# Attention values as unsplit float32 products in the two column halves of the array, 512 queries at a time

## The chip, the cores and the metric

The kernel runs on one core of one Trainium2 chip. The metric is the device time of one execution in microseconds (us); the time before is the median of three runs, 1407.62 us, with 1405.22 us the lowest and 1408.63 us the highest. One further execution was recorded by the hardware profiler, and every row below is from that recording.

## What is computed

One layer of a streaming encoder, for 1024 new frames of one stream (the prompt, `T` = 1024) and for 32 next frames of a running stream (the sample, with 512 cached frames). Cut to the part that the change touches:

```
q, k, v = projections of rmsnorm(x), 16 heads of 64 channels; q and k normed per head
s = q @ k.T + (C[query] - C[key])           # C: cumulative log forget gates
s = where(query >= key, s, -inf); p = softmax(s)
o = p @ v                                    # per head, float32
ya = (o * silu(ga)) @ w_pa                   # beside it: a convolution branch, two gates, w_out
```

The prompt's attention is causal: query block i (128 queries) sees key blocks 0 to i. The running frames attend to the 512 cached keys and their own 32. The projections of q, k, v, of the gates (`ga`, `gb`, `ma`, `mb`) and of the convolution inputs (`ua`, `ub`) are the greater part of the work.

## The kernel before

**Number format.** TensorE is fed with numbers of a reduced float32 format (`F32R`). A float32 operand is split into a high part, rounded to that format, and a low part, the difference. A projection is then three products per tile (high by high, low by high, high by low; `mms`, L97 to L103, all on L102). A few products use plain float32 operands: the running frames' (L541, L860, L861, L895, L897), the column sums (L216, L995) and all transposes.

**Stages.** Up to about 610 us the kernel projects u, v, k, q and `ga` and writes them to scratch in device memory. From there to 1100 us it runs attention (the stretch that the change is about), with 22 of the 24 remaining gate projections between the attention steps as filler (`fill`, `filler`). The rest runs two more gates and then the three output projections.

**Values of the prompt, made once.** In the loop at L575 a 128-token block of v for four heads comes out of PSUM. ScalarE copies it twice: to `vf` (L588, written to the output `vO`) and to the high half of `vb` (L590). Three beats later VectorE forms the low half (`low`, L594), and SyncE writes `vb` to the scratch `s_v` (L597). So `s_v` holds, for each head, 64 high and 64 low columns side by side.

**One attention head.** `Head.load` (L770) loads q and k. `load_v` (L787) loads the head's 8 key blocks of `[high | low]` values into the one buffer `V`; for heads after the first it is called in the main loop when block 7 of the head before is done (L1050). A head is eight blocks; each block goes through three steps:

- `scores` (L906): products of queries and keys into PSUM, the row maximum on VectorE (L922), the exponential on ScalarE (L925), the scaling by the row sum on GpSimd (L928).
- `turn` (L930): up to 8 TensorE transposes (L945) of 128 by 128 pieces of P into PSUM, up to four to a PSUM buffer `ptr2`; then ScalarE casts the buffer to `pth` (high, L949) and VectorE subtracts to get `ptl` (low, L950). Two query blocks share a pair of tiles of 256 queries; GpSimd zeroes the corner above the diagonal in each (L935, L936).
- `values` (L952), only after odd blocks: with the 128 columns `[high | low]` of V as the stationary operand, the 256 queries of `pth` and then of `ptl` stream past, over 2, 4, 6 or 8 key blocks (L961, L962). The upper and the lower 64 rows of `po` are two partial sums; ScalarE copies one (L966), VectorE adds the other (L967), and for odd heads multiplies by the gate (L972) and the result is written to `s_o`.

The transposes and `po` draw on the same three PSUM buffers (`psT`).

**Order.** In attention the order of TensorE's instructions is the order of the program text (`manual_schedule`); the other engines' order is the scheduler's. The main loop (L1035) does, for step n of the list of blocks: scores of step n+3; loads for n+5; `turn` of n; `fill(4)`, that is 12 filler products; `values` of step n-2 if one is due.

**The running frames.** Four `Sample` steps, of four heads each, stand in the list. `Sample.values` (L888) multiplies, for each of its four heads j in turn, four cached key blocks (L895) and the 32 new keys (L897): plain float32, 64 stationary columns, 32 queries, into rows 0 to 63 of PSUM for even j and 64 to 127 for odd j.

Of the kernel before, what the change touches and what calls it, by code (L numbers as in the profile page):

```python
# [15 lines left out]
D = 1024  # L16
# [32 lines left out]
def build(tc, xT, xt, wv, wf, ckT, cv, clT, stT, vec, cst, yT, kT, vO, lfO, cpT, csT):  # L49
# [10 lines left out]
    s_v = dram.tile([8, 128, H, 128], F32, name="s_v")  # L60
# [17 lines left out]
    def f32(ap):  # L78
        return ap.bitcast(F32)
# [481 lines left out]
    for c in range(4):  # L561
        if c == 2:
            pace["rate"] = R_U
            u_proj(2, pj)
            while ("y", 0) not in sides or len(taps) > 62:
                pump(1)

            def shifted():
                shift_of(sides["y", 0])
                taps[:0] = sums(0)  # L570

            later(6, shifted)
        pace["rate"] = R_V
        wh2, wl2 = split.pop(("v", c))
        for t in range(8):  # L575
            ps = pj.tile([128, 512], F32, name="pjv", tag="pj")
            n = 0
            for kt in range(KT):
                sl = slice(t * 128, t * 128 + 128)
                wh, wl = wh2[kt // 4][:, kt % 4, :], wl2[kt // 4][:, kt % 4, :]  # L580
                for a, b in ((xh[:, kt, sl], wh), (xl[:, kt, sl], wh), (xh[:, kt, sl], wl)):
                    nc.tensor.matmul(ps[:, :VC], a, b, start=(n == 0), stop=(n == 23))  # L582
                    n += 1
                beat()
            if t == 2:
                fetch()
            vf = vp.tile([128, 256], F32, name="vf", tag="vf", bufs=6)
            nc.scalar.copy(vf, ps[:, :256])  # L588
            vb = vp.tile([128, 4, 128], F32R, name="vb", tag="vb", bufs=5)
            nc.scalar.copy(vb[:, :, 0:64], ps[:, :256].rearrange("p (h d) -> p h d", h=4))  # L590
            nc.scalar.copy(z[:, t, 4 * c:4 * c + 4], ps[:, 256:260])
            nc.sync.dma_start(vO[t * 128:t * 128 + 128, 256 * c:256 * c + 256], vf)

            def low(ps=ps, vb=vb, t=t, c=c):  # L594
                nc.vector.tensor_sub(vb[:, :, 64:128], ps[:, :256].rearrange("p (h d) -> p h d", h=4),
                                     f32(vb[:, :, 0:64]))
                nc.sync.dma_start(s_v[t, :, 4 * c:4 * c + 4, :], f32(vb))  # L597

            later(3, low)
    pvw.close()  # L600

    fp = pool("fp", 1, stack=pv, side="right")
# [163 lines left out]
    class Head:  # L766
# [3 lines left out]
        def load(self):  # L770
            h = self.h
            self.q = [hp.tile([n, T], F32R, name=a, tag=a) for a, n in (("QA", 68), ("QB", 128), ("KA", 68),
                                                                        ("KB", 128))]
            QA, QB, KA, KB = self.q
            hs = slice(64 * h, 64 * h + 64)
            nc.sync.dma_start(f32(QB[0:64]), s_q[1, hs, :])
            nc.sync.dma_start(f32(QB[64:128]), s_q[0, hs, :])
            nc.sync.dma_start(f32(KB[0:64]), s_k[0, hs, :])
            nc.sync.dma_start(f32(KB[64:128]), s_k[1, hs, :])
            nc.sync.dma_start(f32(QA[0:64]), s_q[0, hs, :])  # L780
            nc.sync.dma_start(f32(QA[64:68]), s_aq[h])
            nc.sync.dma_start(f32(KA[0:64]), s_k[0, hs, :])
            nc.sync.dma_start(f32(KA[64:68]), s_ak[h])
            if h == 0:
                self.load_v()

        def load_v(self):  # L787
            h = self.h
            self.V = hp.tile([128, 8, 128], F32R, name="V", tag="V", bufs=1)
            nc.sync.dma_start(f32(self.V), s_v[:, :, h, :].rearrange("b t d -> t b d"))  # L790

    cvt[0] = u7p
    pace["rate"] = R_U
# [44 lines left out]
    class Sample:  # L838
# [49 lines left out]
        def values(self):  # L888
            vc, vn, pts, g = self.vc, self.vn, self.pts, self.g
            po = psT.tile([128, 512], F32, name="po", tag="T")  # L890
            for j in range(4):
                b0 = 64 * (j % 2)
                o = po[b0:b0 + 64, 32 * (j // 2):32 * (j // 2) + 32]
                for b in range(4):
                    nc.tensor.matmul(o, vc[:, b, 64 * j:64 * j + 64], pts[:, b, 32 * j:32 * j + 32],  # L895
                                     start=(b == 0), stop=False)
                nc.tensor.matmul(o, vn[:, 64 * j:64 * j + 64], pts[:TS, 4, 32 * j:32 * j + 32], start=False, stop=True)  # L897
            nc.vector.tensor_copy(os_t[:, 2 * g:2 * g + 2, :], po[:, :64].rearrange("p (a n) -> p a n", a=2))

    class Block:  # L900
# [28 lines left out]

        def turn(self):  # L930
            i, P = self.i, self.P
            if i % 2 == 0:
                tg = f"{(i // 2) % 2}"
                pth, ptl = [ap.tile([128, i + 2, 256], F32R, name=a, tag=a + tg, bufs=1) for a in ("pth", "ptl")]
                nc.gpsimd.memset(f32(pth[:, i + 1, 0:128]), 0.0)  # L935
                nc.gpsimd.memset(f32(ptl[:, i + 1, 0:128]), 0.0)  # L936
                self.head.p = pth, ptl
            self.p = self.head.p
            pth, ptl = self.p
            qo = slice((i % 2) * 128, (i % 2) * 128 + 128)  # L940
            for u in range((i + 4) // 4):
                nj = min(4, i + 1 - 4 * u)
                pt = psT.tile([128, 512], F32, name="ptr2", tag="T")
                for j in range(nj):
                    nc.tensor.transpose(pt[:, 128 * j:128 * j + 128],  # L945
                                        P[:, 128 * (4 * u + j):128 * (4 * u + j) + 128], ident)
                p3 = pt[:, :128 * nj].rearrange("p (j q) -> p j q", j=nj)
                js = slice(4 * u, 4 * u + nj)
                nc.scalar.copy(pth[:, js, qo], p3)  # L949
                nc.vector.tensor_sub(ptl[:, js, qo], p3, f32(pth[:, js, qo]))  # L950

        def values(self):  # L952
            if self.i % 2 == 0:
                return
            c, e = self.i // 2, self.head.h % 2
            pth, ptl = self.p
            V, ot = self.head.V, self.head.ot
            njb = 2 * c + 2
            po = psT.tile([128, 512], F32, name="po", tag="T")
            for j in range(njb):  # L960
                nc.tensor.matmul(po[:, :256], V[:, j, :], pth[:, j, :], start=(j == 0), stop=False)  # L961
                nc.tensor.matmul(po[:, :256], V[:, j, :], ptl[:, j, :], start=False, stop=(j == njb - 1))  # L962
            osl = slice(c * 256, c * 256 + 256)
            own = slice(64 * e, 64 * e + 64)
            oth = slice(64 - 64 * e, 128 - 64 * e)
            nc.scalar.copy(ot[own, osl], po[oth, :256])  # L966
            nc.vector.tensor_add(ot[own, osl], ot[own, osl], po[own, :256])  # L967
# [5 lines left out]
            if e == 1 and c == 3:  # L973
                nc.sync.dma_start(s_o[self.head.h // 2, :, :T], ot)

    seq = []
    for h in heads:
        seq += [Block(h, i) for i in range(8)]
# [56 lines left out]
    for n, b in enumerate(seq):  # L1035
        if n + 3 < len(seq):
            start(seq[n + 3])
        if n + 5 < len(seq) and getattr(seq[n + 5], "i", 1) == 0:
            seq[n + 5].head.load()
        if n + 6 < len(seq) and isinstance(seq[n + 6], Sample):  # L1040
            seq[n + 6].load()
        if isinstance(b, Sample):
            fill(4)
            b.turn()
        else:
            b.turn()
# [219 lines left out]
```

## Time and profile before

| | |
|---|---|
| Runs | 1407.62 us median of 3 (1405.22 to 1408.63) |
| Span of the profiled execution | 1405.2 us, mean granted TensorE clock 0.998 |
| Busy share of the span: PE, DVE, ACT, POOL | 99%, 67%, 45%, 44% |
| Attention, 610 to 1100 us of the span | PE 486.4 of 490.0 us, DVE 329.0, ACT 266.3, POOL 177.8 |
| Device memory | 142 GB/s over the span, 201 MB |

The page gives the span of the profiled execution, 1405.2 us, and no other time for it; the median of the runs is 2.4 us above the span. PE is TensorE's matmul queue, PEld its loads of stationary operands, DVE VectorE, ACT ScalarE, POOL GpSimd, SP SyncE, whose queue issues the transfers. The duration of a matmul in a row includes its way through the array, in which the next one has already started: what a matmul costs a full TensorE is the distance from its start to the next one's. In an operand such as `128*64 128x32`, the first pair is the rows and columns of the array that are used, the second the streaming operand (rows by columns). In a timeline, neighbouring instructions of one line that touch are merged into one row with their count.

### The profile page before, as it was taken

How to read it: one execution, taken by the hardware profiler on the slowest of the kernel's cores; microseconds unless marked ns; L12 is line 12 of the kernel's file. 1: busy time of each engine (PE TensorE's matmuls, PEld its weight loads, DVE VectorE, ACT ScalarE, POOL GpSimd, SP SyncE). 2: the span in 40 equal slices, each digit the busy share in tenths (PEclk: the TensorE clock that was granted, in tenths of full speed). 3: DMA queues.
4: the chain of work that ended last, by engine and by line, in shares of the span. 5: the costliest groups of instructions: out<-in, count | busy, mean ns of one | idle time of the engine just before them, and what ended most of it. 6: DMA issues, size and time to landing. Idle time of an engine off the chain costs nothing.

```text
span 1405.2 us, 24570 instructions
## 1 busy us (share of the span) xinstructions
PE 1393.8 (99%) x9255; PEld 1363.2 (97%) x9255; DVE 936.7 (67%) x1407; ACT 637.7 (45%) x1308; POOL 624.3 (44%) x665
## 2 busy tenths in 40 slices
PE   9999999999999999999999999999999999999999
PEld 8999999999999999999999999999999999999998
DVE  6688787888898999567677767755565487133111
ACT  6332334645464642255545656654554456232100
POOL 2324254557585875344333434333432267255320
PEclk9999999999999999999999999999999999999999
DMA  4253443424342483343546546453542688444431
GB/s 181 92 178 114 153 134 101 159 84 136 110 146 95 143 200 120 129 123 103 147 123 175 160 138 175 115 164 110 171 132 82 231 286 285 146 138 142 150 108 47
DMA packets 110614, 201.23 MB, mean 143 GB/s; under 512 B 17376, under 2 KB 74592, under 8 KB 110496
## 3 DMA queue, kind: packets, MB, share of 16 engines
q1 hardware_dynamic: 110352, 199.60, 45.4%
q8 instruction: 73, 1.20, 0.4%
q14 instruction: 45, 0.37, 0.1%
q10 hardware_dynamic: 144, 0.07, 0.0%
HBM read 129.78 MB, written 69.84 MB: 142 GB/s over the span
## 4 chain that ended last, share of the span: by engine, by line
PE 93%; DVE 3%; issue 2%; ACT 2%; POOL 1%; ACTq 0%; DVEq 0%; POOLq 0%
PE pj L102 68%; PE pjv L582 7%; PE ptr L945 4%; PE po L961 3%; PE po L962 3%; PE psS L917 2%; PE psS L918 2%; DVE nm L922 1%; PE po L895 1%; PE warm L345 1%; PE pst L706 1%; PE pst L705 1%; POOL wl L94 0%; PE ptx L427 0%; DVE y L258 0%
## 5 line engine op out<-in xcount | busy, mean ns | idle before, releaser
L102 PE MATMUL pj<-xh,wh 128*128 128x352 f32 (+2 forms) x1536 | 510.0, 332 | 3.8 <-ACT t L761 3.5
L102 PE MATMUL pj<-xl,wh 128*128 128x352 f32 (+2 forms) x1536 | 495.3, 322 | 0.2
L102 PE MATMUL pj<-xh,wl 128*128 128x352 f32 (+2 forms) x1536 | 494.0, 322 | 0.2 <-POOL wl L94 0.2
L94 POOL TENSOR_TENSOR wl<-raw,wh 128x384 fp32r<-128x384 f32 (+1 forms) x258 | 319.3, 1266 | 227.7 <-ACT wh L91 208.3
L258 DVE SCALAR_TENSOR_TENSOR y<-u,vec_t,y 128x1086 f32<-128x1086 f32 x240 | 379.6, 1582 | 11.6 <-ACT y L255 8.3
L102 PEld LDWEIGHTS pj<-xh,wh 128*128 128x128 f32 x1536 | 289.3, 188 | 11.8 <-ACT t L761 8.2
L102 PEld LDWEIGHTS pj<-xh,wl 128*128 128x128 f32 x1536 | 289.8, 189 | 0.8 <-POOL wl L94 0.5
L102 PEld LDWEIGHTS pj<-xl,wh 128*128 128x128 f32 x1536 | 289.2, 188 | 1.4 <-DVE xl L430 1.2
L928 POOL TENSOR_SCALAR P<-P,nm 128x128 f32<-128x128 f32 (+7 forms) x128 | 97.8, 764 | 223.7 <-DVE nm L927 190.2
L91 ACT CAST wh<-raw 128x1024 fp32r<-128x1024 f32 x86 | 90.1, 1048 | 111.3 <-PE pj L102 80.0
L925 ACT ACTIVATE P<-psS,nm 128x128 f32<-128x128 f32 (+7 forms) x128 | 95.7, 748 | 66.7 <-DVE nm L922 61.4
L949 ACT CAST pth<-ptr 128x512 fp32r<-128x512 f32 (+1 forms) x192 | 86.1, 484 | 74.3 <-PE ptr L945 73.3
L950 DVE TENSOR_TENSOR ptl<-ptr,pth 128x512 fp32r<-128x512 f32 (+1 forms) x192 | 100.7, 549 | 13.8 <-ACT pth L949 12.4
L922 DVE TENSOR_REDUCE nm<-psS 128x1 f32<-128x128 f32 (+7 forms) x128 | 96.5, 754 | 5.7
L723 POOL TENSOR_TENSOR ql<-qn,qh 128x352 fp32r<-128x352 f32 (+1 forms) x48 | 65.7, 1370 | 69.3 <-ACT qh L722 55.5
L945 PE MATMUL ptr<-ident,P 128*128 128x128 f32 x576 | 85.0, 274 | 0.0
L961 PE MATMUL po<-pth,V 128*128 128x256 f32 x320 | 79.2, 283 | 0.0
L962 PE MATMUL po<-ptl,V 128*128 128x256 f32 x320 | 78.6, 281 | 0.0
L945 PEld LDWEIGHTS ptr<-ident,P 128*128 128x128 f32 x576 | 69.8, 141 | 5.2
L920 DVE TENSOR_TENSOR psS<-psS,cmask 128x128 f32<-128x128 f32 x128 | 37.7, 294 | 54.3 <-PE psS L918 53.0
L582 PE MATMUL pjv<-vwh,xh 128*128 128x260 f32 x256 | 72.5, 283 | 0.0
L582 PE MATMUL pjv<-vwl,xh 128*128 128x260 f32 x256 | 72.4, 283 | 0.0
(205 smaller groups left out, 2518.5 us busy)
## 6 DMA issues: line engine op xcount, KB each, us to landing
raw<-wf SPq DMA_DIRECT2D x88, 512.0 KB
s_v<-vb SPq DMA_DIRECT2D x32, 256.0 KB
QB<-s_q SPq DMA_DIRECT2D x32, 256.0 KB
KB<-s_k SPq DMA_DIRECT2D x32, 256.0 KB
V<-s_v SPq DMA_DIRECT2D x16, 512.0 KB
kT<-qn SPq DMA_DIRECT2D x8, 528.0 KB
s_ga<-t SPq DMA_DIRECT2D x24, 176.0 KB
s_gb<-t SPq DMA_DIRECT2D x24, 176.0 KB
```

What stands on the lines that cost most here:

```text
L91: nc.scalar.copy(wh, raw)
L94: nc.gpsimd.tensor_sub(wl[:, k0:k1, :], raw[:, k0:k1, :], f32(wh[:, k0:k1, :]))
L102: nc.tensor.matmul(ps, a[:, kt, :], b(kt, sl), start=(first and n == 0), stop=(last and n == N - 1))
L258: t = nc.vector.scalar_tensor_tensor(y, u[:, i:i + CW], w, y, op0=ALU.mult, op1=ALU.add)
L582: nc.tensor.matmul(ps[:, :VC], a, b, start=(n == 0), stop=(n == 23))
L922: nc.vector.tensor_reduce(nm[:, 0:1], ps[:, :nb, :w], axis=AX.XY, op=ALU.max, negate=True)
L925: nc.scalar.activation(P[:, :nk].rearrange("p (b w) -> p b w", b=nb), ps[:, :nb, :w], AF.Exp, bias=nm[:, 0:1], accum_out=nm[:, 1:2])
L928: nc.gpsimd.tensor_scalar(P[:, :nk], P[:, :nk], nm[:, 2:3], 1.0, op0=ALU.mult, op1=ALU.mult)
L945: nc.tensor.transpose(pt[:, 128 * j:128 * j + 128], P[:, 128 * (4 * u + j):128 * (4 * u + j) + 128], ident)
L950: nc.vector.tensor_sub(ptl[:, js, qo], p3, f32(pth[:, js, qo]))
L961: nc.tensor.matmul(po[:, :256], V[:, j, :], pth[:, j, :], start=(j == 0), stop=False)
L962: nc.tensor.matmul(po[:, :256], V[:, j, :], ptl[:, j, :], start=False, stop=(j == njb - 1))
```

## The change

It makes four edits.

1. **Values stay whole.** `vb`, `low` and its delay go; `s_v` is `[8, 128, 1024]` and the same `vf` that is written to the output is written to it (128 KB a time in place of 256 KB).
2. **Heads in pairs.** `load_v` and its place in the main loop go. The load of an even head brings the values of both heads of the pair as one 512 KB transfer at the end of that head's loads, into a tile with two buffers.
3. **`turn` and `values` by 512 queries.** Two tiles that live through the whole stage take P transposed, as plain float32: `PT[0]` for query blocks 0 to 3 (4 key blocks), `PT[1]` for 4 to 7 (8 key blocks). Their corners are zeroed once, ahead of the loop. `turn` makes one copy of each PSUM buffer, on ScalarE for the first four key blocks and on VectorE for the others; nothing is subtracted. `values` runs only after blocks 3 and 7. Its key blocks go in pairs: the even one's values (64 stationary columns of the head) write rows 0 to 63 of `po`, the odd one's rows 64 to 127. The last pair streams only the 256 queries that it concerns. The two halves of `po` are summed as before, 512 queries at a time.
4. **`Sample.values`** takes the two heads of a PSUM column group together: for each key block, first one head, then the other.

```diff
-            vb = vp.tile([128, 4, 128], F32R, name="vb", tag="vb", bufs=5)
-            nc.scalar.copy(vb[:, :, 0:64], ps[:, :256].rearrange("p (h d) -> p h d", h=4))
             nc.scalar.copy(z[:, t, 4 * c:4 * c + 4], ps[:, 256:260])
             nc.sync.dma_start(vO[t * 128:t * 128 + 128, 256 * c:256 * c + 256], vf)
...
-            later(3, low)
+            nc.sync.dma_start(s_v[t, :, 256 * c:256 * c + 256], vf)
...
-            if h == 0:
-                self.load_v()
...
+            if h % 2 == 0:
+                self.V = heads[h + 1].V = hp.tile([128, 8, 128], F32, name="V", tag="V")
+                nc.sync.dma_start(self.V, s_v[:, :, 64 * h:64 * h + 128].rearrange("b t d -> t b d"))
...
+            for p in range(2):
+                for b in range(5):
+                    for j in (2 * p, 2 * p + 1):
+                        o = po[64 * (j % 2):64 * (j % 2) + 64, 32 * p:32 * p + 32]
+                        js, qs = slice(64 * j, 64 * j + 64), slice(32 * j, 32 * j + 32)
+                        v, t = (vc[:, b, js], pts[:, b, qs]) if b < 4 else (vn[:, js], pts[:TS, 4, qs])
+                        nc.tensor.matmul(o, v, t, start=(b == 0), stop=(b == 4))
...
-                nc.scalar.copy(pth[:, js, qo], p3)
-                nc.vector.tensor_sub(ptl[:, js, qo], p3, f32(pth[:, js, qo]))
+                put = nc.vector.tensor_copy if u else nc.scalar.copy
+                put(pt_[:, 4 * u:4 * u + nj, qo], pt[:, :128 * nj].rearrange("p (j q) -> p j q", j=nj))
...
-            for j in range(njb):
-                nc.tensor.matmul(po[:, :256], V[:, j, :], pth[:, j, :], start=(j == 0), stop=False)
-                nc.tensor.matmul(po[:, :256], V[:, j, :], ptl[:, j, :], start=False, stop=(j == njb - 1))
+            for j in range(0, njb, 2):
+                q0 = 256 if j == njb - 2 else 0
+                for o in range(2):
+                    nc.tensor.matmul(po[64 * o:64 * o + 64, q0:], V[:, j + o, hd], p[:, j + o, q0:],
+                                     start=(j == 0), stop=(j == njb - 2), skip_group_check=True)
...
+    PT = [ap.tile([128, 4 * n, 512], F32, name=f"pt{n}", bufs=1) for n in (1, 2)]
+    for n, pt_ in enumerate(PT):
+        for j in range(4 * n, 4 * n + 4, 2):
+            nc.gpsimd.memset(pt_[:, j + 1, 128 * (j % 4):128 * (j % 4) + 128], 0.0)
...
-        return isinstance(b, Sample) or b.i % 2
+        return isinstance(b, Sample) or b.i % 4 == 3
...
-        if n >= 2 and getattr(seq[n - 2], "i", 0) == 7 and seq[n - 2].head.h + 1 < H:
-            heads[seq[n - 2].head.h + 1].load_v()
```

More of the change, by code (lines that the diff above doesn't have):

```diff
@@ L59, in build @@
     s_k = dram.tile([2, D, T], F32, name="s_k")
-    s_v = dram.tile([8, 128, H, 128], F32, name="s_v")
+    s_v = dram.tile([8, 128, D], F32, name="s_v")
     s_vs = dram.tile([TS, D], F32, name="s_vs")
@@ L588, in build @@
             nc.scalar.copy(vf, ps[:, :256])
-            vb = vp.tile([128, 4, 128], F32R, name="vb", tag="vb", bufs=5)
-            nc.scalar.copy(vb[:, :, 0:64], ps[:, :256].rearrange("p (h d) -> p h d", h=4))
             nc.scalar.copy(z[:, t, 4 * c:4 * c + 4], ps[:, 256:260])
             nc.sync.dma_start(vO[t * 128:t * 128 + 128, 256 * c:256 * c + 256], vf)
[L594 to L597, printed above, removed]
-            later(3, low)
+            nc.sync.dma_start(s_v[t, :, 256 * c:256 * c + 256], vf)
     pvw.close()
@@ L783, in load @@
             nc.sync.dma_start(f32(KA[64:68]), s_ak[h])
-            if h == 0:
-                self.load_v()
[L787 to L790, printed above, removed]
+            if h % 2 == 0:
+                self.V = heads[h + 1].V = hp.tile([128, 8, 128], F32, name="V", tag="V")
+                nc.sync.dma_start(self.V, s_v[:, :, 64 * h:64 * h + 128].rearrange("b t d -> t b d"))
     cvt[0] = u7p
@@ L890, in values @@
             po = psT.tile([128, 512], F32, name="po", tag="T")
[L891 to L897, printed above, removed]
+            for p in range(2):
[5 more added lines that the diff above has]
+                        nc.tensor.matmul(o, v, t, start=(b == 0), stop=(b == 4))
             nc.vector.tensor_copy(os_t[:, 2 * g:2 * g + 2, :], po[:, :64].rearrange("p (a n) -> p a n", a=2))
@@ L931, in turn @@
             i, P = self.i, self.P
[L932 to L940, printed above, removed]
+            pt_ = PT[i // 4]
+            qo = slice((i % 4) * 128, (i % 4) * 128 + 128)
             for u in range((i + 4) // 4):
@@ L946, in turn @@
                                         P[:, 128 * (4 * u + j):128 * (4 * u + j) + 128], ident)
[L947 to L950, printed above, removed]
+                put = nc.vector.tensor_copy if u else nc.scalar.copy
+                put(pt_[:, 4 * u:4 * u + nj, qo], pt[:, :128 * nj].rearrange("p (j q) -> p j q", j=nj))
         def values(self):
[L953 to L958, printed above, removed]
-            po = psT.tile([128, 512], F32, name="po", tag="T")
-            for j in range(njb):
-                nc.tensor.matmul(po[:, :256], V[:, j, :], pth[:, j, :], start=(j == 0), stop=False)
-                nc.tensor.matmul(po[:, :256], V[:, j, :], ptl[:, j, :], start=False, stop=(j == njb - 1))
-            osl = slice(c * 256, c * 256 + 256)
+            c, e = self.i // 4, self.head.h % 2
+            V, ot, p = self.head.V, self.head.ot, PT[self.i // 4]
+            hd = slice(64 * e, 64 * e + 64)
+            njb = 4 * c + 4
+            po = psT.tile([128, 512], F32, name="po", tag="T")
+            for j in range(0, njb, 2):
[3 more added lines that the diff above has]
+                                     start=(j == 0), stop=(j == njb - 2), skip_group_check=True)
+            osl = slice(c * 512, c * 512 + 512)
             own = slice(64 * e, 64 * e + 64)
             oth = slice(64 - 64 * e, 128 - 64 * e)
-            nc.scalar.copy(ot[own, osl], po[oth, :256])
-            nc.vector.tensor_add(ot[own, osl], ot[own, osl], po[own, :256])
+            nc.scalar.copy(ot[own, osl], po[oth, :])
+            nc.vector.tensor_add(ot[own, osl], ot[own, osl], po[own, :])
             if e == 1:
@@ L972, in values @@
                 nc.vector.tensor_mul(ot[:, osl], ot[:, osl], self.head.g[:, osl])
-            if e == 1 and c == 3:
+            if e == 1 and c == 1:
                 nc.sync.dma_start(s_o[self.head.h // 2, :, :T], ot)
+    PT = [ap.tile([128, 4 * n, 512], F32, name=f"pt{n}", bufs=1) for n in (1, 2)]
+    for n, pt_ in enumerate(PT):
+        for j in range(4 * n, 4 * n + 4, 2):
+            nc.gpsimd.memset(pt_[:, j + 1, 128 * (j % 4):128 * (j % 4) + 128], 0.0)
     seq = []
```

## The prediction

> **What bounds the kernel now.** I read the page first, then the busy times by stage, then TensorE's own waits.
>
> ```profile
> PE 1393.8 (99%) x9255; PEld 1363.2 (97%) x9255; DVE 936.7 (67%) x1407; ACT 637.7 (45%) x1308; POOL 624.3 (44%) x665
> PE 93%; DVE 3%; issue 2%; ACT 2%; POOL 1%; ACTq 0%; DVEq 0%; POOLq 0%
> ```
> ```profile
> 610.00:1100.00 490.00, 486.44 (x3389) 466.53 (x3388) 328.98 (x756) 266.25 (x627) 177.83 (x315) 0.99 0.48 136
> ```
> ```profile
> engine line waited for: us in total, times, longest us
> PE pj L102 <- ACT t L761: 3.5, 10, 0.4
> ...
> PE pj L102 <- POOL wl L94: 0.2, 1, 0.2
> PE psS L917 <- ACT P L925: 0.2, 1, 0.2
> ```
>
> TensorE is busy for 99% of the span, and for 486.4 of the 490.0 us of attention (columns after the window: its length, then busy us of PE, PEld, DVE, ACT, POOL, then the granted clock). In all of attention it waits under 4 us, never for a transpose buffer, for `po` or for V. So this stage lasts as long as TensorE's own list of instructions, and an edit counts for what it does to that list. A high busy share doesn't say that TensorE works at its peak, so I cost its instructions by the distance between starts.
>
> **The products of the prompt's values.** They lie in edit 3. Before, the last head (the products after blocks 5 and 7, 12 and 16 of them, happen to touch):
>
> ```profile
> 1096.57 0.28 PE L961 MATMUL po<-pth,V 128*128 128x256 f32 x1
> ...
> 1099.77 0.28 PE L962 MATMUL po<-ptl,V 128*128 128x256 f32 x1
> 1099.89 0.33 PE L102 MATMUL pj<-xh,wh 128*128 128x352 f32 x1
> ```
>
> 28 products in 1099.89 - 1096.57 = 3.32 us, 0.1186 us each. A head has 2 x (2 + 4 + 6 + 8) = 40, sixteen heads 640: **75.9 us**.
>
> After, each product is plain float32. What such a product costs, and whether two halves of the array work at the same time, no value product of before shows, but other float32 products do:
>
> ```profile
> L995 PE MATMUL psn<-mean,ones_f x6: 459/459/471, 854.1 to 858.8; 128*128 128x352 f32 x6
> ```
> ```profile
> 854.06 0.76 PE L995 MATMUL psn<-mean,ones_f 128*128 128x352 f32 x2
> ```
> ```profile
> 687.31 0.28 PE L962 MATMUL po<-ptl,V 128*128 128x256 f32 x1
> 687.52 1.08 PE L860 MATMUL psS<-kc,qs_t 64*32 64x512 f32 x8
> 688.40 0.26 PE L861 MATMUL psS<-ks_t,qs_t 64*32 64x32 f32 x8
> ```
> ```profile
> 68.38 0.32 PE L102 MATMUL pj<-xl,wh 128*128 128x352 f32 x1
> 68.64 1.09 PE L541 MATMUL pjs<-vraw,xsm 128*32 128x260 f32 x16
> 69.65 0.43 PE L102 MATMUL pj<-xh,wh 128*128 128x352 f32 x1
> ```
>
> L995 is one product per column chunk (three of them), yet six instructions: a float32 product is two passes. The two end 0.76 us after the first began and one lasts 0.459, so a pass of 352 columns takes 0.30 us, 0.85 ns a column, when alone in the array. L541 issues 16 passes of 260 columns, four to each quarter of the array's columns, over all 128 rows and each quarter with a stream of its own. One after the other they would take 16 x 0.22 = 3.5 us; from first start to the next instruction it is 1.01 us, about four passes. L860 says the same for 512 columns: eight passes in four tiles, 0.88 us, so 0.44 us a pass with four at a time. I take it that two halves run side by side as four quarters do, at 0.43 us per pass of 512 and 0.22 per pass of 256 (0.44 holds the filling of the first pass, which I count with the next term). That term is the change of the array's shape: from L102 at 68.38 to L102 at 69.65 are 1.27 us; less 0.16 for the product at 68.38 (starts of L102 lie 0.16 apart) and 4 x 0.217 for the passes, 0.24 us remain for going in and out. Before, value products pay none of it.
>
> Queries 0 to 511 are a pair of passes of 512 and a pair of 256: 2 x 0.43 + 2 x 0.22 + 0.24 = 1.54 us. Queries 512 to 1023 have three full pairs: 6 x 0.43 + 2 x 0.22 + 0.24 = 3.26 us. Per head 4.80, sixteen heads **76.8 us: 0.9 us more** than before. For the same reason as before, two passes at half speed in two halves are what two products of the split were in the whole array; only the shape changes are new. With 0.44 a pass it would be +2.2, with 0.20 for a block's changes of shape -0.4.
>
> **The running frames' values (edit 4).**
>
> ```profile
> 709.11 0.32 PE L102 MATMUL pj<-xl,wh 128*128 128x352 f32 x1
> 709.37 0.65 PE L895 MATMUL po<-pts,vc 128*64 128x32 f32 x8
> 709.95 0.30 PE L897 MATMUL po<-pts 32*64 32x32 f32 x2
> 710.18 0.65 PE L895 MATMUL po<-pts,vc 128*64 128x32 f32 x8
> ...
> 712.38 0.30 PE L897 MATMUL po<-pts 32*64 32x32 f32 x2
> 712.60 0.47 PE L917 MATMUL psS<-KB,QB 128*128 128x448 f32 x1
> ```
>
> Four heads in turn, each in one half of the array while the other stands idle: 0.58 us for the eight passes of L895 and 0.23 for L897, 3.23 us for the block. After, two heads alternate in the two halves: each stretch should take what one head took, twice instead of four times, 1.62 us. Four such blocks save 4 x 1.61 = **6.5 us**. The lower bound is that only the number of shape changes falls and the loads of the stationary columns, which set the pace here, take turns: an eight-pass stretch then stays 0.58 less the 0.12 that I put on its shape change, 0.46 a head, so 2 x (2 x 0.46 + 0.12 + 0.33) = 2.74 us and 2.0 us in all. I take the upper value, because L861 starts eight short passes, loads included, within 0.26 us.
>
> **TensorE's clock.** Two stretches of 3.41 us have half the clock:
>
> ```profile
> 709.37:712.60 3.23, 3.23 (x41) 1.00 0.00 0
> 713.55:716.96 3.41, 3.41 (x14) 0.50 0.87 304
> 836.42:839.83 3.41, 3.41 (x23) 1.00 0.41 138
> 955.87:959.28 3.41, 3.41 (x23) 1.00 0.39 143
> 1078.78:1082.19 3.41, 3.41 (x13) 0.50 0.64 223
> ```
> ```profile
> 831.87 0.65 PE L895 MATMUL po<-pts,vc 128*64 128x32 f32 x8
> ```
> ```profile
> 951.28 0.65 PE L895 MATMUL po<-pts,vc 128*64 128x32 f32 x8
> ```
> ```profile
> 1075.64 0.65 PE L895 MATMUL po<-pts,vc 128*64 128x32 f32 x8
> ```
>
> Both come right behind a block of L895. They lie 365.23 us apart, 107 times 3.413, so I read them as cells of a fixed grid, each set by what the cell before it held. Blocks one and four fill 2.46 and 3.14 us of the cell before; blocks two and three (from 831.87 and 951.28, same length) straddle a boundary of that grid and fill at most 2.1 us of a cell, and no slow stretch follows. A block of 1.6 us stays below all of these, so both slow stretches should go: half of 3.41 us, twice, **3.4 us**. The Trainium skill, "TensorE: Matmul & The Clock Gate", section "Why this matters for your kernels", asks only for no idle gap above about 3 us between bursts; PE shows none here, so by that rule the slow stretches have another cause and would stay. That is the third rival.
>
> **What lies off TensorE's path.** The rows of what `turn`, the sums and V cost:
>
> ```profile
> L949 ACT CAST pth<-ptr 128x512 fp32r<-128x512 f32 x96 | 54.9, 589 | 53.2 <-PE ptr L945 52.8
> ```
> ```profile
> L950 DVE TENSOR_TENSOR ptl<-ptr,pth 128x512 fp32r<-128x512 f32 x96 | 64.5, 684 | 13.6 <-ACT pth L949 12.4
> L967 DVE TENSOR_TENSOR ot<-ot,po 64x256 f32<-64x256 f32 x64 | 26.7, 417 | 53.9 <-ACT ot L966 53.3
> ```
> ```profile
> SPq L790 <- PE po L962: 28.2, 10, 8.2
> ```
>
> A full transpose buffer was held for 0.59 us of ScalarE and then 0.68 of VectorE, and is now held for one copy. The sums of `po` are half as many and twice as wide, so `po` is held somewhat longer, with the 12 filler products (1.9 us) and more between two uses. ScalarE and VectorE lose work; TensorE waited for neither, so I cost this at nothing. It is worth at most the 3.5 us that TensorE waits for ScalarE's copies of the filler (L761). The new tiles `PT` could make the copies of a head wait for the value products of the head before; the `values` call of block 3 comes three steps before the next head's first copy, and likewise for `PT[1]`; a step is 490/132 = 3.7 us, so some 11 us cover it. SyncE's queue no longer stands behind V's single buffer (28.2 us, waited out with nothing on TensorE behind it), and the earlier V load queues behind the same head's other loads, five steps ahead. The shorter work on v ends in a stage where TensorE doesn't wait either. After the last value products come two gates of 72 products, 144 x 0.16 = 23 us, which cover the longer last sum.
>
> **Sum.** +0.9 - 6.5 - 3.4 = -9.0 us in the profiled execution, 1405.2 to 1396.2. Taken off the median: **1398.6 us**. The case's own range is 1393 (less the 3.5 us of waits for ScalarE, 1.3 for cheaper changes of shape, and rounded) to 1402.
>
> **Rivals.**
> - *The second half starts a pass late.* The Trainium skill, same page, section "Part 3: Packing small matmuls", says matmuls start and end strictly in program order. The two passes of the even key block stand ahead of the odd block's, so the odd half would first begin with the even half's second pass. Once running, nothing more is lost; each of the 32 value blocks ends one pass later, 32 x 0.43 = 13.8 us: 1412.4, slower. It decides as soon as more than 9.0/32 = 0.28 us per block is lost. Against it: in the program each head's L861 follows its L860, yet the rows have all eight L860 ahead of all L861, done in 0.88 us where strict order would need over three.
> - *The halves take turns.* 16 x (8 x 0.43 + 4 x 0.22) = 69 us more: 1468. L541 speaks against it.
> - *The slow stretches stay*: 1398.6 + 3.4 = 1402.0. For it: two of four blocks had none behind them.
> - *The loads of stationary columns take turns* in `Sample.values`: blocks of 2.74 us still bring slow stretches: +0.9 - 2.0 = -1.1, 1406.5.
> - *Something waits anew* (a buffer, ScalarE's order): a few us either way about the forecast.
>
> **Chances.** Forecast 0.66; slow stretches stay 0.09; loads in turns 0.10; second half late 0.06; halves in turns 0.04; a new wait 0.05. A measurement can tell about 0.3%, 4.2 us, from no change. Faster by over that (under 1403.4): the forecast, nearly all of the third rival, 0.74. Within: the loads in turns and parts of the others, 0.14. Slower: 0.12. The range 1393 to 1408 takes in the forecast's own, the third and fourth rivals and the spread of the runs above them (1.0 us); it leaves out the two rivals on the slow side and part of the last, under 0.2.
>
> **What would show it.** 384 value matmuls in place of 640, in rows of `128*64 128x512`, a head's pair of blocks in about 4.8 us of starts; the four passes of a full pair within 0.9 us, the two halves starting nearly together; blocks of L895's successor of 1.6 us; no stretch of half clock in attention; attention about 481 us long; no new PE wait. It would be wrong if value blocks show gaps of 0.43 us, if slow stretches come behind the new float32 blocks of 3.3 us, or if TensorE waits for the copies to `PT`.

## The result, and the profile after

The changed kernel takes 1402.99 us (median of 5 runs, 1401.52 to 1405.11); the kernel before, in the same session, 1407.62 us (5 runs, 1405.22 to 1409.06). The ratio is 0.9969, 95% interval 0.9957 to 0.9982: 4.6 us faster, about half of the 9.0 us forecast. The execution that the profiler recorded is the slowest of the five, 1405.11 us with a span of 1403.3 us, so in the traces the span falls by only 1.9 us (1405.2 before).

The page of the changed kernel, busy time and the chain that ended last:

```profile
PE 1390.1 (99%) x8999; PEld 1303.6 (93%) x8999; DVE 866.0 (62%) x1199; ACT 604.2 (43%) x1180; POOL 617.5 (44%) x541
PE 92%; issue 3%; DVE 2%; ACT 2%; POOL 1%; DMA 1%; SPq 0%; ACTq 0%; POOLq 0%; DVEq 0%
```

VectorE lost 71 us of work, ScalarE 34. TensorE is still what the end waits for, so these savings count only where it waited for these engines. For ScalarE's copies of the filler it waited 3.5 us before; now it waits 1.7:

```profile
PE pj L102 <- ACT t L753: 1.1, 2, 0.8
PE psS L905 <- ACT t L751: 0.6, 1, 0.6
```

The timeline of TensorE in the changed kernel: the two value blocks of the last head, each with the row that follows it, and the first sample block.

```profile
1084.68 1.51 PE L940 MATMUL po<-pt,V 128*64 128x512 f32 x8
1086.13 0.98 PE L926 MATMUL ptr<-ident,P 128*128 128x128 f32 x7
...
1091.75 3.23 PE L940 MATMUL po<-pt,V 128*64 128x512 f32 x16
1094.91 0.43 PE L102 MATMUL pj<-xh,wh 128*128 128x352 f32 x1
```
```profile
712.06 0.66 PE L885 MATMUL po<-pts,vc 128*64 128x32 f32 x16
...
713.47 0.30 PE L885 MATMUL po<-pts 32*64 32x32 f32 x4
713.70 0.47 PE L905 MATMUL psS<-KB,QB 128*128 128x448 f32 x1
```

What was costed came out nearly as costed. A head's value blocks take 1.45 and 3.16 us from their first start to the next instruction, and each is entered about 0.09 us late; the forecast had 1.54 and 3.26 with entering included. One piece is missing from it: the instruction behind a block of the new shape takes longer too. Behind the last filler product above (1099.89 us before, 1094.91 after) the next one starts 0.17 us later before and 0.27 after:

```profile
1100.06 0.32 PE L102 MATMUL pj<-xh,wl 128*128 128x352 f32 x1
```
```profile
1095.18 0.32 PE L102 MATMUL pj<-xh,wl 128*128 128x352 f32 x1
```

The sample block takes 713.70 - 712.06 = 1.64 us (forecast 1.62), and no stretch of half clock follows any of the four.

The last value product is followed by a filler product at 1099.89 us before and at 1094.91 after: 5.0 us of the 9.0 are there at the end of attention, and 3.1 of these are gone by the end of the span. The other 4 us were mostly lost ahead of attention: from one and the same filler product at 597.09 us before and 600.55 after, the way to this point is 8.4 us shorter. In TensorE's list of waits a new line shows where to look (0.2 us, once, before):

```profile
PE pj L102 <- POOL wl L94: 3.4, 4, 1.9
```

TensorE waits four times for the low halves of a projection's weights, which GpSimd makes. One of these waits lies just ahead of attention, three behind it.

**Ahead of attention.** The row at which TensorE waits, in the kernel before and in the changed one:

```profile
589.34 0.43 PE L102 MATMUL pj<-xh,wl 128*128 128x352 f32 x1 [0.20 <-POOL wl L94]
```
```profile
591.23 0.43 PE L102 MATMUL pj<-xh,wl 128*128 128x352 f32 x1 [1.94 <-POOL wl L94]
```

Followed backwards: GpSimd starts these low halves at 588.27 us before and at 590.18 after, because it first adds a square that ScalarE delivers 1.93 us later; ScalarE has it from VectorE, whose queue has run late since a subtraction (L228) that waited for the store `s_y` some 55 us earlier. SyncE's queue there, before and after:

```profile
517.66 0.26 SPq L783 DMA_DIRECT2D KA<-s_ak  x1
520.48 0.37 SPq L288 DMA_DIRECT2D cpT<-u  x1
...
525.97 0.38 SPq L222 DMA_DIRECT2D s_y<-y  x1
```
```profile
519.10 0.26 SPq L775 DMA_DIRECT2D KA<-s_ak  x1
521.62 0.39 SPq L778 DMA_DIRECT2D V<-s_v  x1
...
527.46 0.32 SPq L222 DMA_DIRECT2D s_y<-y  x1
```

And VectorE's subtraction, which has to wait until that store has read `y`, before and after:

```profile
529.94 1.33 DVE L228 TENSOR_TENSOR y<-y,shift 128x1024 f32<-128x1024 f32 x2 [2.40 <-DMA s_y<-y]
```
```profile
532.35 1.33 DVE L228 TENSOR_TENSOR y<-y,shift 128x1024 f32<-128x1024 f32 x2 [4.68 <-DMA s_y<-y]
```

The V at 521.62 is that of the second pair. In the program text its load stands five steps ahead of head 2; but its buffer is the second of two and waits for nothing, so the scheduler put it directly behind the loads of head 1, ahead of the stores. The wait has a tail. Windows of the changed kernel (length; busy us of PE, PEld, DVE, ACT, POOL; granted clock; DMA share; GB/s):

```profile
589.03:592.44 3.41, 1.47 (x9) 1.21 (x8) 0.00 (x0) 1.58 (x3) 3.41 (x5) 1.00 0.74 190
592.44:595.85 3.41, 3.41 (x14) 3.41 (x13) 0.00 (x0) 0.00 (x0) 3.41 (x8) 0.50 0.99 353
```

TensorE stood still for 1.94 us of one cell of the clock's grid, and the next cell of 3.41 us has half the clock: 1.7 us more.

**Behind attention.** GpSimd's queue, before and after (`wl` low halves of weights, `c_l` low half of a channel of the convolution branch):

```profile
1140.60 3.48 POOL L1109 TENSOR_TENSOR c_l<-y,c_h 128x1056 fp32r<-128x1056 f32 x1
1146.39 2.48 POOL L1109 TENSOR_TENSOR c_l<-y,c_h 128x1056 fp32r<-128x1056 f32 x1 [2.31 <-ACT c_h L1108]
1150.64 4.72 POOL L94 TENSOR_TENSOR wl<-raw,wh 128x384 fp32r<-128x384 f32 x3 [1.76 <-ACT wh L91]
```
```profile
1135.88 3.48 POOL L1090 TENSOR_TENSOR c_l<-y,c_h 128x1056 fp32r<-128x1056 f32 x1
1143.86 6.06 POOL L1090 TENSOR_TENSOR c_l<-y,c_h 128x1056 fp32r<-128x1056 f32 x2 [4.50 <-ACT c_h L1089]
1149.87 5.73 POOL L94 TENSOR_TENSOR wl<-raw,wh 128x384 fp32r<-128x384 f32 x3
...
1176.25 4.79 POOL L94 TENSOR_TENSOR wl<-raw,wh 128x384 fp32r<-128x384 f32 x3 [3.55 <-issue]
```

Before, two `c_l` and then a set of weights; after, three `c_l` come first (one at 1135.88, two in the row at 1143.86). Measured from the start of the last value product (1099.77 and 1094.60 us) the weights start 50.9 us later before and 55.3 us after; the later sets follow late, and TensorE waits in the first output projection. Between 1176 and 1203 us five distances between starts of L102 are 0.32 to 1.13 us instead of 0.16, 2.5 us too much in sum; the two largest waits behind them:

```profile
1177.39 0.43 PE L102 MATMUL pj<-ah,wl 128*128 128x352 f32 x1 [0.54 <-POOL wl L94]
1202.83 0.43 PE L102 MATMUL pj<-ah,wl 128*128 128x352 f32 x1 [0.70 <-POOL wl L94]
```

So the theory after the result: the three costed terms hold in their sum, and the shortfall consists in the main of two losses off TensorE's own list, the early V load ahead of attention (1.7 us, with the slow cell 3.4) and GpSimd's order behind it (2.5 us). In the profiled execution that is 5.9 of the 7.1 us by which the span misses the forecast. The slow cell is not in every execution: the granted clock is 0.999 in two of the five runs, the profiled one among them, and 1.000 in three. Without it the two losses are 4.2 us, and the medians miss 4.4. The rivals: a value block costs more than forecast; or the losses come from TensorE being earlier, whatever the order.

### The profile page after: what moved, and what is told of

It is laid out like the page before. It is cut to its first block, busy times and chain, and to the rows that moved or that the text cites. A ratio compares the mean times of both kernels' runs of the same rounds, so it can differ in the third digit from the quotient of the medians.

```text
span 1403.3 us, 23422 instructions
## 1 busy us (share of the span) xinstructions
PE 1390.1 (99%) x8999; PEld 1303.6 (93%) x8999; DVE 866.0 (62%) x1199; ACT 604.2 (43%) x1180; POOL 617.5 (44%) x541
## 4 chain that ended last, share of the span: by engine, by line
PE 92%; issue 3%; DVE 2%; ACT 2%; POOL 1%; DMA 1%; SPq 0%; ACTq 0%; POOLq 0%; DVEq 0%
PE pj L102 67%; PE pjv L582 7%; PE po L940 5%; PE ptr L926 4%; PE psS L905 3%; PE psS L906 2%; POOL wl L94 1%; PE pst L698 1%; PE pst L697 1%; PE po L885 0%; DVE y L1082 0%; PE ptx L427 0%; DMA xtok<-xt 0%; ACT xh L429 0%; PE pjs L541 0%
## 5 line engine op out<-in xcount | busy, mean ns | idle before, releaser
L102 PE MATMUL pj<-xh,wh 128*128 128x352 f32 (+2 forms) x1536 | 510.0, 332 | 1.7 <-ACT t L753 1.1
L102 PE MATMUL pj<-xh,wl 128*128 128x352 f32 (+2 forms) x1536 | 494.0, 322 | 1.9 <-POOL wl L94 1.9
L102 PE MATMUL pj<-xl,wh 128*128 128x352 f32 (+2 forms) x1536 | 495.5, 323 | 0.2
L94 POOL TENSOR_TENSOR wl<-raw,wh 128x384 fp32r<-128x384 f32 (+1 forms) x258 | 323.1, 1280 | 258.1 <-ACT wh L91 226.9
L102 PEld LDWEIGHTS pj<-xh,wh 128*128 128x128 f32 x1536 | 289.0, 188 | 10.2 <-ACT t L753 6.6
L102 PEld LDWEIGHTS pj<-xh,wl 128*128 128x128 f32 x1536 | 289.9, 189 | 2.5 <-POOL wl L94 2.2
L102 PEld LDWEIGHTS pj<-xl,wh 128*128 128x128 f32 x1536 | 289.1, 188 | 1.4 <-DVE xl L430 1.2
L916 POOL TENSOR_SCALAR P<-P,nm 128x128 f32<-128x128 f32 (+7 forms) x128 | 107.6, 842 | 283.3 <-DVE nm L915 216.9
L929 ACT COPY pt<-ptr 128x512 f32<-128x512 f32 (+3 forms) x128 | 65.0, 508 | 75.8 <-PE ptr L926 75.1
L940 PE MATMUL po<-pt,V 128*64 128x512 f32 (+1 forms) x384 | 75.8, 530 | 0.0
L582 PE MATMUL pjv<-vwh,xl 128*128 128x260 f32 x256 | 72.3, 282 | 0.0
L905 PE MATMUL psS<-KB,QB 128*128 128x256 f32 (+2 forms) x192 | 70.1, 366 | 0.6 <-ACT t L751 0.6
```

The costliest lines, as they stand in the source:

```text
L94: nc.gpsimd.tensor_sub(wl[:, k0:k1, :], raw[:, k0:k1, :], f32(wh[:, k0:k1, :]))
L102: nc.tensor.matmul(ps, a[:, kt, :], b(kt, sl), start=(first and n == 0), stop=(last and n == N - 1))
L905: nc.tensor.matmul(ps[:, b, :wm], QB[:, qsl], KB[:, ksl], start=True, stop=False)
L916: nc.gpsimd.tensor_scalar(P[:, :nk], P[:, :nk], nm[:, 2:3], 1.0, op0=ALU.mult, op1=ALU.mult)
L940: nc.tensor.matmul(po[64 * o:64 * o + 64, q0:], V[:, j + o, hd], p[:, j + o, q0:], start=(j == 0), stop=(j == njb - 2), skip_group_check=True)
```

## Experiments

| Run | What differs | Median us (range, runs) | Ratio to before, 95% |
|---|---|---|---|
| a_v_late | after, pair's V in one buffer, loaded late | 1401.50 (1400.41 to 1402.50, 5) | 0.9968, 0.9956 to 0.9980 |
| b_sample | before, edit 4 only | 1397.71 (1397.43 to 1398.55, 5) | 0.9942, 0.9931 to 0.9954 |
| a_no_sample | after without edit 4 | 1411.64 (1409.93 to 1415.50, 6) | 1.0037, 1.0026 to 1.0049 |
| a_v_late_ln | a_v_late, layer-norm channels moved | 1402.17 (1401.44 to 1403.62, 7) | 0.9973, 0.9962 to 0.9983 |
| a_order | a_v_late, GpSimd's order of before | 1399.40 (1398.80 to 1399.72, 5) | 0.9942, 0.9928 to 0.9956 |
| a_early_order | after, GpSimd's order of before | 1400.53 (1399.98 to 1401.31, 5) | 0.9959, 0.9944 to 0.9974 |
| b_extra_load | before, one unused 512 KB load | 1405.91 (1404.81 to 1409.70, 11) | 0.9995, 0.9985 to 1.0006 |
| b_extra_3 | before, three unused loads | 1413.27 (1411.03 to 1414.17, 6) | 1.0045, 1.0029 to 1.0061 |
| a_one_half | a_order, both key blocks in one half | 1466.40 (1466.37 to 1466.43, 2) | 1.0419, 1.0399 to 1.0440 |

The first four shared a chip and a session with before at 1405.57 us (13 runs), a_order, b_extra_load and a_one_half one with before at 1406.66 us (14 runs), the last two of the text below (a_early_order, b_extra_3) one with before at 1406.69 us (11 runs).

**The V load late again (a_v_late).**

```diff
-            if h % 2 == 0:
-                self.V = heads[h + 1].V = hp.tile([128, 8, 128], F32, name="V", tag="V")
-                nc.sync.dma_start(self.V, s_v[:, :, 64 * h:64 * h + 128].rearrange("b t d -> t b d"))
+            if h == 0:
+                self.load_v()
+
+        def load_v(self):
+            h = self.h
+            self.V = heads[h + 1].V = hp.tile([128, 8, 128], F32, name="V", tag="V", bufs=1)
+            nc.sync.dma_start(self.V, s_v[:, :, 64 * h:64 * h + 128].rearrange("b t d -> t b d"))
...
+        if n >= 2 and getattr(seq[n - 2], "i", 0) == 7 and seq[n - 2].head.h % 2 and seq[n - 2].head.h + 1 < H:
+            heads[seq[n - 2].head.h + 1].load_v()
```

> The changed kernel with one difference: V of a pair has one buffer again and its load is issued in the main loop when block 7 of the odd head before is done. Theory (the second V load, free to go early, stands ahead of the s_y store at 521.6 us, and the delay runs through VectorE, ScalarE and GpSimd to TensorE at 589 us): the s_y store goes out about 2.3 us earlier, the wait of 1.9 us on wl at 589 us falls to about 0.2, no stretch of half clock follows it, and the median is 2 to 3 us below 1403.0. Rival (the delay comes from the new PT tiles or from the other order of stores of v): the wait at 589 us stays at about 1.9 us and the median within 1 us of 1403.

The store `s_y` is issued at 525.74 us, VectorE's subtraction starts at 529.91, the wait at 589 us is gone, and so is the slow cell behind it (span 1398.6 us in the profile). The rival is out, since the new tiles and the other stores of v are in this kernel too. The medians differ by 1.5 us between sessions and the ratios not at all (0.9968 and 0.9969): the mechanism is shown by the trace, its price not by this pair.

**The sample edit alone (b_sample).** The kernel before with the loop of edit 4 and nothing else.

> The kernel before with the new order in Sample.values alone. Forecast's steps: blocks of 1.6 us in place of 3.2, no stretch of half clock behind them, so 6.5 us from the blocks and up to 3.4 from the clock: median 1397.7 to 1401. Rival 1 (the clock stretches have another cause): they stay, 1401. Rival 2 (whatever attention gains is partly given back in the stage after it, where GpSimd's low halves of the weights come late): attention 6.5 to 10 us shorter, but 2 to 3 us of new TensorE waits on wl after 1140 us, median 1400 to 1404.

By the medians it takes 7.9 us off, and its profiled span is 1395.6 us, 9.6 below that of before; the two costed terms of this edit were 6.5 + 3.4 = 9.9. The granted clock is 1.000 in all five runs, against 0.995 to 0.999 for before. Both rivals are out: no stretch of half clock is left in attention, and TensorE waits for no low half of weights. This one loop is worth nearly as much as the whole forecast, and this is the kernel with the lowest median of the study.

**The change without the sample edit (a_no_sample).**

> The changed kernel with Sample.values as before: the values edit alone. Forecast's steps: value products +0.9 us on the kernel before, and the stretches of half clock behind the samples' blocks stay, so 1408.5 with nothing else; with the late s_y store of the changed kernel 2 to 3 us more, 1410 to 1412. If the waits after attention are a fixed order and not a matter of TensorE's earliness, they are here too, 3 us: 1413. If they come from TensorE being early, they are absent.

It is slower than before, by 6.1 us. Three of its four sample blocks have stretches of half clock behind them, one of two cells:

```profile
713.58:720.41 6.83, 6.83 (x26) 6.39 (x25) 3.02 (x5) 1.89 (x4) 1.69 (x2) 0.50 0.51 156
839.87:843.28 3.41, 3.41 (x14) 3.18 (x13) 1.40 (x3) 1.16 (x2) 0.00 (x0) 0.50 0.49 154
1085.63:1089.04 3.41, 3.41 (x15) 3.34 (x13) 1.55 (x3) 1.68 (x3) 0.12 (x1) 0.50 0.85 269
```

In the profile, which is that of the slowest of its six runs, it is 8.5 us longer than before. Twice as many cells (four instead of two) make 3.4 us, the longer wait at 589 us 2.0, the waits of the first output projection 2.3, the value products 3.1 (worked out below), and 2.0 us of waits for ScalarE fall away: 8.8. So the sample block is what brings the slow cells; how many depends on where the blocks lie on the grid, and an edit elsewhere that shifts them changes the count. In the four profiles with the old block (before, a_no_sample, b_extra_load, b_extra_3) nine of the 16 blocks put 2.46 to 3.17 us into one cell of the grid, and a slow cell follows each of them; seven put at most 2.25 us into any cell, and none follows. Why two cells follow the first block here is not shown. And TensorE reaches the first output projection 6 us later than in before and still loses time there, while in b_sample it reaches it 9.5 us earlier and loses none: the rival that TensorE's earliness makes the waits is out.

**The layer norm's channels dealt out otherwise (a_v_late_ln).**

```diff
-LNO = ((0,), (1, 2), (3,), (4, 5), (6,), (7,), ())
+LNO = ((0,), (1,), (2,), (3, 4), (5,), (6,), (7,))
```

> a_v_late with the channels of the convolution branch spread otherwise over the steps of the first output projection (0; 1; 2; 3 and 4; 5; 6; 7 in place of 0; 1 and 2; 3; 4 and 5; 6; 7; none). If the waits on wl after 1140 us come from the low halves of the weights standing behind this branch's work in ScalarE's and GpSimd's order, another spread moves them: fewer waits than the 3 us of the changed kernel, median 1 to 3 us below a_v_late. If they come from the total of that work, they stay or grow, since the last channel is ready later.

A miss: the order of GpSimd's queue behind attention came out as in a_v_late, so nothing was tested.

**GpSimd's order of before (a_order).** On top of a_v_late the third channel's halves are made to follow the weights, by two dependencies and another dealing of the channels:

```diff
-LNO = ((0,), (1, 2), (3,), (4, 5), (6,), (7,), ())
+LNO = ((0,), (1,), (), (2, 3), (4, 5), (6,), (7,))
...
+            done_w[0] = nc.scalar.copy(wh, raw)
+                done_w[1] = nc.gpsimd.tensor_sub(wl[:, k0:k1, :], raw[:, k0:k1, :], f32(wh[:, k0:k1, :]))
...
+            if f == 2:
+                behind_w.enter_context(tc.issue_after(done_w[0].ins))
             nc.scalar.copy(chl[0][:, f, :], y)
...
+            if f == 2:
+                behind_w.enter_context(tc.issue_after(done_w[1].ins))
             nc.gpsimd.tensor_sub(chl[1][:, f, :], y, f32(chl[0][:, f, :]))
```

> The changed kernel with the pair's V loaded late, and after attention GpSimd's order of before: the low half of the convolution branch's third channel behind the weights of the first output projection's third step, instead of ahead of them. Nothing in attention differs from the run with V loaded late (1401.5 us). Theory (the 2 to 3 us of gaps behind attention come from this order of GpSimd's queue): the gaps of the matmul queue in front of L102 between 1165 and 1200 us go, 1399 to 1399.5 us, within 2 us of the kernel before with the sample edit alone (1397.7). Rival (the gaps come from something else that the edit of the values brings, such as the longer last sum or the earlier end of TensorE's work): the gaps stay, 1401.5.

1399.40 us, 2.1 below a_v_late by the medians of two sessions on one chip, 3.7 by the ratios. In the profiles, from the 2,800th projection product to the end of the span, it is 1.5 us (810.91 and 809.40 us). GpSimd's queue, and no wait of L104 (the former L102) for it from 570 to 1200 us:

```profile
1141.00 2.60 POOL L1104 TENSOR_TENSOR c_l<-y,c_h 128x1056 fp32r<-128x1056 f32 x1 [4.50 <-ACT c_h L1100]
1143.56 5.74 POOL L96 TENSOR_TENSOR wl<-raw,wh 128x384 fp32r<-128x384 f32 x3
1149.26 6.95 POOL L1104 TENSOR_TENSOR c_l<-y,c_h 128x1056 fp32r<-128x1056 f32 x2
```

The order was the second loss. The edit moves ScalarE's half of the channel as well as GpSimd's, so it shows the order of the two together. With both losses mended the change gives 0.9942, applied to 1407.62 us 1399.5 (1397.5 to 1401.4); the forecast was 1398.6.

**The early load with the order mended (a_early_order).** The edit of a_order on the changed kernel, V loaded early.

> The changed kernel with GpSimd's order of before behind attention, as in the run that gave 1399.4 us, but with the pair's V loaded early, as the change has it. Theory (two losses that add up: 1.5 to 2 us by the early load ahead of attention, about 2 us by GpSimd's order behind it): 1401 to 1401.5 us, TensorE waits 1.9 to 2.2 us for the low halves of a filler weight near 589 us, and no gaps in front of L102 between 1165 and 1200 us. Rival (the early load costs nothing, as the run with one unused load more in the kernel before says, and the whole of the shortfall lies behind attention): 1399.4 us.

1400.53 us, between the rival and the theory. The wait at 589 us is there, at 1.05 us shorter than in the changed kernel:

```profile
590.64 0.43 PE L104 MATMUL pj<-xh,wl 128*128 128x352 f32 x1 [1.05 <-POOL wl L96]
```

The early load costs 1.1 us by medians, 2.4 by the ratios (0.9959 and 0.9942, whose intervals overlap) and 1.0 in the profiles from the 2,800th projection product on; no slow cell follows this shorter wait. The loss is smaller than I expected: here `s_y` is issued at 526.80 us, 0.7 earlier than in the changed kernel, with the same instructions ahead of it on the queue. The price of this loss is 1 to 2 us and not known better.

**An early load in the kernel before (b_extra_load).**

```diff
+            if h == 1:
+                with tc.issue_after(last.ins):
+                    nc.sync.dma_start(s_x, s_v[:, :, 2, :].rearrange("b t d -> t b d"))
```

`last` is the load `KA<-s_ak` of head 1; `s_x` is a scratch that nobody reads.

> The kernel before, with one 512 KB transfer more, from the scratch of v to an unused scratch in device memory, put on SyncE's queue where the changed kernel has the early load of the second pair's V (behind the last load of head 1, ahead of the stores of the layer norm's input); nobody reads it, and every engine's order is otherwise that of before. Theory (the early load delays the store s_y, and with it VectorE, ScalarE, GpSimd and the low halves of a filler weight): TensorE waits for those low halves about 1.9 us at 589 us, where it waits 0.2 in the profile of before, and the kernel takes 1.7 to 3.5 us longer than before, 1407.3 to 1409 on the chip of the first runs. Rival (the load alone is harmless, the wait comes with the new zeroing of the corners on GpSimd or another step of the change): no new wait, no difference.

No difference, and 0.2 us of wait at 589: my theory fell in the form in which it stood. The queue shows why:

```profile
520.32 0.60 SPq L789 DMA_DIRECT2D s_x<-s_v  x1
521.49 0.36 SPq L289 DMA_DIRECT2D cpT<-u  x1
...
525.79 0.43 SPq L223 DMA_DIRECT2D s_y<-y  x1
```

The load moved the issue behind it by 1.0 us, but the store stood at its data: two stores of the gates' results ahead of it had a stretch of 1.87 us in before, and take 0.80 here. One load fills a slack and no more. In the changed kernel `KA<-s_ak` is already 1.4 us late, so I take the slack to have been used up when V took its place.

**Three loads (b_extra_3).** The same with `for x in range(3)`.

> The kernel before with three unused loads of 512 KB instead of one, all ahead of the store s_y on SyncE's queue. One of them moved every issue behind it by 1.0 to 1.2 us, which the store took up without coming later (525.97 us in the profile of before, 525.79 with the load): its data came no sooner. In the changed kernel a load of head 1 lands about 1.3 us later as well, and its store is 1.5 us late. Theory (the cost is the place in the queue, once its slack of about 1.2 us is used up): with three, the store is issued near 528 us, TensorE waits 2 to 3 us for the low halves of the filler weight near 589 us, and the kernel takes 2 to 4.5 us longer than before. Rival (the early load is harmless; the wait in the changed kernel comes from other steps of it): no new wait, no difference from before.

6.6 us slower, direction right and price beyond what I expected. The store comes 2.8 us late, ScalarE's and GpSimd's halves of the weights after it:

```profile
528.73 0.53 SPq L223 DMA_DIRECT2D s_y<-y  x1
```
```profile
591.55 0.43 PE L103 MATMUL pj<-xh,wh 128*128 128x352 f32 x1 [0.84 <-ACT wh L92]
594.21 0.43 PE L103 MATMUL pj<-xh,wl 128*128 128x352 f32 x1 [2.23 <-POOL wl L95]
```

That is 3.1 us, then a cell at half clock (1.7 us), and 1.7 us lost near 543 us, which I had not foreseen. So a place in the queue ahead of `s_y` is what costs, once the slack is gone.

**Both key blocks in one half (a_one_half).**

```diff
-                    nc.tensor.matmul(po[64 * o:64 * o + 64, q0:], V[:, j + o, hd], p[:, j + o, q0:],
-                                     start=(j == 0), stop=(j == njb - 2), skip_group_check=True)
+                    nc.tensor.matmul(po[0:64, q0:], V[:, j + o, hd], p[:, j + o, q0:],
+                                     start=(j + o == 0), stop=(j + o == njb - 1), skip_group_check=True)
...
-            nc.scalar.copy(ot[own, osl], po[oth, :])
-            nc.vector.tensor_add(ot[own, osl], ot[own, osl], po[own, :])
+            nc.scalar.copy(ot[own, osl], po[0:64, :])
```

There is one sum in one half of the array, so the sum of the two halves is left out.

> As the run with GpSimd's order of before, but both key blocks of a pair write the same 64 columns of the array (rows 0 to 63 of po, one accumulation over all key blocks, no sum of two halves): the same 384 value matmuls, the same result, never two halves at a time. Theory (the two halves run side by side): the passes of a pair take turns, 8 x 0.43 + 4 x 0.22 = 4.3 us a head more, 9.1 us in place of 4.8, in all 69 us: about 1468 us. Rival (passes in two halves take turns already, and a pass is cheaper than I costed it): no difference. Rival (the second half starts a pass late): 69 - 14 = 55 us more.

67.0 us slower than a_order (69 expected). The same value products, the last head:

```profile
1144.18 2.79 PE L946 MATMUL po<-pt,V 128*64 128x512 f32 x8
1146.90 0.98 PE L932 MATMUL ptr<-ident,P 128*128 128x128 f32 x7
...
1152.52 6.23 PE L946 MATMUL po<-pt,V 128*64 128x512 f32 x16
1158.68 0.43 PE L104 MATMUL pj<-xh,wh 128*128 128x352 f32 x1
```

2.72 and 6.16 us a head in place of 1.45 and 3.16. Two halves run side by side; no pass is lost at their start.

## Why the prediction was wrong

- *Value products, +0.9 us: held in the sum, by luck.* From the 2,800th projection product to the end of the span (ahead of it the two profiles differ by a slow cell near 20 us) a_order takes 1397.93 - 588.53 = 809.40 us and b_sample 1395.64 - 587.19 = 808.45: +0.95 for everything but the sample edit. But the starts of TensorE's instructions in these two traces show two parts. The 32 value blocks take 73.6 us, entering them 3.4 and the longer instruction behind them 2.9, 79.8 us in all against 76.7 in b_sample: +3.1. The forecast's 0.24 us for a change of shape ended at the start of the next instruction and left out the 0.10 that this one takes longer. Against it, TensorE's waits in this stretch fall from 4.2 to 1.7 us, most of it for ScalarE's copies of the filler, which the forecast put at nothing. The two errors nearly cancel.
- *The second half a pass late, and halves in turns: out.* The Trainium skill, "TensorE: Matmul & The Clock Gate", section "Part 3: Packing small matmuls", has matmuls start and end in program order. Taken pass by pass, as the rival took it, the blocks would have been longer by 13.8 us in all. The blocks' 1.45 and 3.16 us leave no room for it, and a_one_half shows what turns cost.
- *The running frames' values, -6.5 us: held* (1.64 us a block, 1.62 forecast). The lower bound of 2.74 us is out.
- *The slow cells, -3.4 us: held* for those behind sample blocks. a_no_sample has four cells where before has two: two was the count of one execution, so the size of this term is that execution's.
- *What lies off TensorE's path, costed at nothing: this step failed.* It said that V's earlier load "queues behind the same head's other loads, five steps ahead", and of the stage behind attention only that 23 us of gates "cover the longer last sum". I looked for waits that the change removes or adds on the instructions it touches, in the order of the program text. The load moved in front of a store that has nothing to do with V, and the scheduler gave GpSimd another order 50 us behind the last touched instruction. Both ended in the same place, the low halves of weights, whose margin the profile of before gave in one line that I quoted as proof of no wait: 0.2 us, once. In place of nothing, the profile of the changed kernel shows 1.7 us more of waiting at 589 us and 2.5 us behind attention, 4.2 of the 4.4 us that the medians miss. The last rival ("something waits anew") had this, at "a few us either way" and 0.05. The range up to 1408 holds the 1402.99 us by luck: it reaches that far for two other rivals, the slow stretches that stay and the loads in turns, and neither came true.
- *Sum.* 9.0 forecast, 4.6 measured; mending both places gives 8.2 by the ratio (6.2 to 10.1) and 7.3 by the medians of that session.

Open is why the loads of head 1 are issued later in every kernel with whole values: the issue of `KA<-s_ak` comes 1.6 to 2.3 us behind that of `KA<-s_k` in seven kernels that have them, 1.0 to 1.1 in the four that don't. The other layout of `s_v` is a candidate that I didn't try. Open too is what led the scheduler to another order behind attention.

## What to carry to other kernels

A wait of 0.2 us on a full engine is a margin of zero: follow its chain back, and ask of every transfer and every step that the scheduler may place freely whether it can come ahead of something on that chain. A buffer added so that a load needs no wait also lets that load go first, so fix its place as well. And when one change holds several edits, time each alone: here a reordered loop of seven lines had all of the gain, and the large edit, with both losses mended, gained nothing: against b_sample it cost 1.7 us by the medians of two sessions, 0.95 in the profiles and nothing by the ratios.

## What the runs showed of the hardware

- The clock. An idle TensorE of 1.94 us within one cell of 3.41 us was followed by a cell at half speed, and so was one of 2.46 us in b_extra_3; in a_no_sample a wait of 2.21 us fell across a boundary (1.53 us in one cell, 0.68 in the next) and none followed. The Trainium skill, "TensorE: Matmul & The Clock Gate", section "Part 1: The HAM clock gate", describes a free-running window of 3413 ns; the 3.413 us grid agrees. The Trainium skill, same page, section "Why this matters for your kernels", allows gaps up to about 3 us; here less was enough, so the measurement decides. A sample block of before, products of 32 columns, that filled 2.46 us or more of a cell also brought a slow cell, with no idle time; 2.25 us or less did not.
- These cells are, as far as the mean clock tells, much of the scatter: before ranges over 5.1 us in 13 runs (clock 0.995 to 0.999), b_sample over 1.1 us in five (clock 1.000).
- Two float32 products in the two column halves take the time of one: a head's blocks take 4.61 us in two halves and 8.88 in one, 68 us for 16 heads, and the median rose by 67.0.
- SyncE's issues stand mostly 1.0 to 1.3 us apart between 520 and 525 us, while the DMA engines are full (share 1.02 to 1.09 from 510 to 525 us in before): one more load there moved the next issue by 1.0 us in b_extra_load.
